# Pairs of experts with at most 32 tokens: 32 slots on four column groups in place of 64 on two

## The chip, the core and the metric

The kernel runs on one core of a Trainium2 chip. The metric is the device time of one execution in microseconds (us). Before the change three runs gave 617.89, 619.68 and 620.88 us; the median is 619.68.

The engines go by the profile's names: PE is the matrix engine and PEld its weight load, DVE, ACT and POOL are the vector, scalar and GpSimd engines, SP issues most DMAs. A letter q behind a name (PEq, PEldq, SPq) is the engine's own sequencer, which fetches and issues its instructions.

## The reference, cut to what matters

The kernel computes one layer over 256 tokens of width 1024. The change touches only its last part, a mixture of 16 experts of inner width 512. A router picks one of four groups of four experts for each token, and two experts in it:

```python
scores = jax.nn.sigmoid(h @ router_w)
sel = scores + router_bias
grp = sel.reshape(sel.shape[:-1] + (N_GROUPS, EXPERTS_PER_GROUP))        # 4 x 4
g_idx = jnp.argmax(jnp.sum(lax.top_k(grp, TOP_K)[0], axis=-1), axis=-1)  # TOP_K = 2
...                                        # e_idx: the two best experts of that group
gate = ...                                 # their scores, normalised, 0 for the others
for e in range(N_EXPERTS):
    he = jax.nn.silu(h @ w1[e]) * (h @ w3[e])
    out = out + gate[..., e:e + 1] * (he @ w2[e])
```

and the layer ends with `xl = xl + g2 * out`. The kernel computes each expert only for the tokens that chose it. With the reference's inputs the fuller expert of each pair (experts 2p and 2p + 1 are pair p) has 55, 42, 15, 14, 49, 72, 29 and 41 tokens, for pairs 0 to 7.

## The kernel before

The part before the experts (up to some 372 us) stays as it is. The experts are worked through in eight pairs. An expert of a pair has 64 slots, so that the 128 partitions hold both: `slots(p, oh, w)` (L1137) makes from a one-hot matrix the slots' transpose `oT` and the gates `gsl` of the slots. `open_group` gathers the tokens of two pairs (`gather`, L1107). Then a pair goes through these steps on PE, each with its line in the rows below:

- `product(p, i, ph)`, L1153 to L1164, the projection w1 (i = 0) or w3 (i = 1): for 8 chunks k of the width and both experts s a matmul with 64 columns (the slots), 512 wide, which fills 64 of 128 partitions of a PSUM bank;
- `silu` on ACT and `weigh` on DVE (gate times silu times the other projection) give `he`; `hidden` (L1173) transposes it on PE;
- `rows` (L1180): the expert outputs, 16 matmuls with 64 columns, 512 wide; `split_rows` writes them as two float32r parts `ys` (ACT and DVE);
- `scatter` (L1190): 16 matmuls with `oT` bring the outputs to the tokens, and DVE adds them to `xl`.

Where an expert has more than 64 tokens, `extra(p, n)` (L1204) does the whole pair again for 32 further slots, with its own matmuls of 32 columns (`phe`, `pye`), and `further` (L1315) repeats this up to 256. Whether this is needed is decided on the chip: `count(p)` (L1308) loads the fuller expert's count from `cnt` into registers of every engine, and `tc.If(counts[p] > 64)` branches on it. `expect(p)` (L1311) puts an early notice of the branch's likely way into PE's stream (BRANCH_PREFETCH_HINT). For pairs 2 to 6 `second` (L1326) puts the second projection into both arms of that branch. So `extra` lies between the branch and the other arm, and a pair that doesn't need it jumps over it.

The order of work on PE is the order of the code (`manual_schedule`); the other engines are ordered by the scheduler. In the loop over p the transposed steps of pair p lie between those of pair p + 1: after the second projection come pair p + 1's slots (and, for odd p, the next group's gather), then `hidden` and `rows` of pair p, two k steps of pair p + 1's first projection, the scatter of pair p, the count, a k step, the notice, and the other five k steps.

The experts' weights are 192 tiles of 512 KB, 24 a pair, in the order of use (`ew_order`, L102). They go through 35 buffers. `load_experts` (L117) issues loads as long as `room` allows, the first 31 on POOL's queue and the others on SP's. `freed(n)` (L1347) gives buffers back in the program's text, 8 for each of a pair's three matrices; a load then still waits on the chip for the matmuls that read its buffer. In pairs 2 to 6 `freed(16)` stands behind the branch, which every engine passes.

PSUM has two pools of banks here: `mm_bank` for projections and half of the transposes, `ax_bank` for the others, with `py` among them.

Pair 7 has its weights cut in another way (`quarter`), so that its products are 256 wide and its outputs come in four quarters (`last_rows(c)`, L1419), each followed by the scatter and the store of the quarter before.

## Time and profile before

| what | value |
| --- | --- |
| median of three runs | 619.68 us (617.89 to 620.88) |
| the profiled execution's own time | 616.12 us |
| its span (first to last instruction) | 614.3 us |
| PE busy | 580.2 us, 94% of the span, 4127 matmuls |
| PEld busy | 408.1 us, 66% |
| DVE / ACT / POOL busy | 349.1 us, 57% / 259.8 us, 42% / 19.4 us, 3% |
| granted PE clock | full in every slice |
| DMA over the span | 170.65 MB, mean 278 GB/s |
| DMA in the expert part | some 407 GB/s in most slices, with a dip to 226 in the one from 538 to 553 us |
| loads of expert weights | 161 on SP's queue (median 10.2 us to landing), 31 on POOL's (7.3 us) |

The profile is one execution; its own time lies 3.6 us under the median of the runs. The rows below are of four kinds. A timeline row is a run of equal instructions of an engine, with its start, its duration and in brackets the idle time before it and what ended that. A windows row gives each engine's busy time in a stretch, the clock, and the share of the stretch in which the 16 DMA engines were busy. A source or tile row lists the instructions of a line or on a tile with least, median and longest duration in ns and the first and last start. And a waits row sums the idle time by what ended it.

### The profile page before, as it was taken

What the parts mean: (1) busy time and instruction counts of PE and PEld (TensorE: products, weight loads), DVE (VectorE), ACT (ScalarE), POOL (GpSimd) and SP (SyncE); (2) the same over time, 40 slices, a digit from 0 to 9 for tenths busy, and PEclk for the clock granted to TensorE, in tenths of its full rate; (3) what the DMA queues carried; (4) which work ended last, traced back from release to release, by engine and by line L of the source; (5) the groups of instructions that cost most, each with busy time, mean ns of one, the idle gap of its engine ahead of it and who ended that gap; (6) DMA issues with size and microseconds to landing.
All of it is one profiled execution on the core that took longest, in us unless ns stands there. A gap on an engine that the chain in (4) does not pass through costs nothing. (4 is left out here: it accounts for less than half of the span.)

```text
span 614.3 us, 10619 instructions
## 1 busy us (share of the span) xinstructions
PE 580.2 (94%) x4127; PEld 408.1 (66%) x4127; DVE 349.1 (57%) x797; ACT 259.8 (42%) x456; POOL 19.4 (3%) x42
## 2 busy tenths in 40 slices
PE   1899999999999899999999988999999999999986
PEld 0789888778788778888899975335445334454454
DVE  4667899999758968988469554121240314132303
ACT  4345446654598765877545624203012111130101
POOL 0000000000000000103112010000000000000000
PEclk9999999999999999999999999999999999999999
DMA  8983874446853463759969776999999999969961
GB/s 256 367 339 114 310 259 154 137 141 193 278 212 103 138 241 103 236 176 356 313 211 379 283 245 226 388 360 406 402 393 407 407 408 409 398 226 409 409 248 68
DMA packets 51825, 170.65 MB, mean 278 GB/s; under 512 B 5664, under 2 KB 10016, under 8 KB 51744
## 3 DMA queue, kind: packets, MB, share of 16 engines
q1 hardware_dynamic: 46704, 151.26, 67.2%
q0 software_dynamic: 5040, 18.35, 8.6%
q8 instruction: 46, 0.75, 0.5%
q14 instruction: 35, 0.29, 0.1%
HBM read 168.54 MB, written 1.05 MB: 276 GB/s over the span
## 5 line engine op out<-in xcount | busy, mean ns | idle before, releaser
L1162 PE MATMUL ph<-ew,xg 128*64 128x512 f32 (+1 forms) x576 | 115.6, 548 | 3.5 <-PEq L1318 2.8
L73 ACT ACTIVATE w<-raw 128x1024 fp32r<-128x1024 f32 x68 | 71.8, 1056 | 65.6 <-PE gps L69 11.6
L74 DVE TENSOR_TENSOR w<-raw,w 128x1024 fp32r<-128x1024 f32 x68 | 82.9, 1219 | 21.5 <-ACT w L73 20.8
L1162 PEld LDWEIGHTS ph<-ew,xg 128*64 128x64 f32 x576 | 41.5, 137 | 66.0 <-issue 58.3
L70 PE MATMUL gps<-h,w 128*128 128x256 f32 x192 | 55.2, 288 | 1.2 <-DVE w L74 1.2
L68 PE MATMUL gps<-h,w 128*128 128x256 f32 x192 | 56.0, 291 | 0.4 <-DVE y L934 0.4
L69 PE MATMUL gps<-h,w 128*128 128x256 f32 x192 | 54.5, 284 | 0.0
L593 DVE SCALAR_TENSOR_TENSOR cacc<-up,vc,cacc 128x243 f32<-128x243 f32 (+14 forms) x120 | 52.1, 472 | 1.4 <-ACT cacc L585 0.7
L1171 DVE SCALAR_TENSOR_TENSOR he<-sl,gsl,ph 128x256 f32<-128x256 f32 x16 | 7.1, 477 | 77.5 <-PE ph L1162 76.2
L1183 PE MATMUL py<-ew,heT 128*64 128x512 f32 x224 | 49.6, 595 | 1.2 <-ACT heT L1178 0.8
L74 DVE TENSOR_TENSOR ys<-py,ys 128x512 fp32r<-128x512 f32 (+1 forms) x18 | 11.4, 633 | 58.0 <-ACT ys L73 58.0
L68 PEld LDWEIGHTS gps<-h,w 128*128 128x128 f32 x192 | 36.6, 191 | 4.2 <-issue 2.6
L70 PEld LDWEIGHTS gps<-h,w 128*128 128x128 f32 x192 | 36.7, 191 | 2.8 <-issue 1.5
L69 PEld LDWEIGHTS gps<-h,w 128*128 128x128 f32 x192 | 36.7, 191 | 0.9 <-issue 0.7
L1183 PEld LDWEIGHTS py<-ew,heT 128*64 128x64 f32 x224 | 15.5, 137 | 30.8 <-issue 26.0
L1201 DVE SCALAR_TENSOR_TENSOR xl<-scp,g,xl 128x256 f32<-128x256 f32 x72 | 29.2, 475 | 7.5 <-PE scp L1197 7.5
L1167 ACT ACTIVATE sl<-ph 128x512 f32<-128x512 f32 (+1 forms) x9 | 5.0, 550 | 63.1 <-PE ph L1162 40.4
L73 ACT ACTIVATE ys<-py 128x512 fp32r<-128x512 f32 (+1 forms) x18 | 9.9, 550 | 50.5 <-PE py L1183 36.6
L114 POOL DMA_DIRECT2D ew<-in_w_exp x31 | 16.6, 537 | 321.1 <-ACT pp L813 248.8
L1119 ACT ACTIVATE xg<-gps,b2m 128x256 f32<-128x256 f32 x32 | 13.4, 471 | 22.7 <-PE gps L1115 21.8
L349 PE MATMUL mps<-ma,cs 128*32 128x256 f32 (+1 forms) x160 | 10.1, 397 | 13.2 <-DMA ma<-in_mod_a 13.1
L1197 PEld LDWEIGHTS scp<-oT,ys 128*128 128x128 f32 x128 | 15.7, 188 | 6.7 <-issue 5.2
(358 smaller groups left out, 1310.0 us busy)
## 6 DMA issues: line engine op xcount, KB each, us to landing
ew<-in_w_exp SPq DMA_DIRECT2D x161, 512.0 KB, 10.2
raw<-in_w_in SPq DMA_DIRECT2D x40, 512.0 KB, 4.4
ew<-in_w_exp POOLq DMA_DIRECT2D x31, 512.0 KB, 7.3
raw<-in_mod_b SPq DMA_DIRECT2D x28, 512.0 KB, 4.1
ma<-in_mod_a SPq DMA_DIRECT2D x12, 512.0 KB, 10.0
raw<-in_w_br SPq DMA_DIRECT2D x12, 512.0 KB, 4.0
raw<-in_w_out SPq DMA_DIRECT2D x8, 512.0 KB, 7.5
ma<-in_mod_a SPq DMA_DIRECT2D x8, 256.0 KB, 6.7
```

The lines of the kernel that those rows point to most:

```text
L68: pe.matmul(ps, wh, xh, start=start, stop=False, skip_group_check=True)
L69: pe.matmul(ps, wh, xl_, start=False, stop=False, skip_group_check=True)
L70: return pe.matmul(ps, wl, xh, start=False, stop=stop, skip_group_check=True)
L73: act.activation(hi, src, AF.Copy)
L74: dve.tensor_tensor(lo, src, r32(hi), op=ALU.subtract)
L114: queue.dma_start(t, w_exp[6 * p + 2 * i + s, :, 1024 * q:1024 * q + 1024])
L593: dve.scalar_tensor_tensor(cacc[:, b, i0:i1], up[:, b, i0 + o:i1 + o], half_d[:, b * 31 + j:b * 31 + j + 1], cacc[:, b, i0:i1], op0=ALU.mu ...
L1119: act.activation(place(k0 + j), ps[:, j, :], AF.Identity, bias=b2m[:, k0 + j:k0 + j + 1])
L1162: pe.matmul(ph[64 * s:64 * s + 64, cols], xg(k)[:, c:c + 64], w[:, at], start=k == 0 and not h, stop=k == KD - 1, skip_group_check=True)
L1183: pe.matmul(py[q][64 * s:64 * s + 64, :], heT[f // 2][:, f % 2, 64 * s:64 * s + 64], ew[p][2][f][s][:, q * 512:q * 512 + 512], start=f == ...
L1197: pe.matmul(ps[:, j, :], rows_(i, m), toks(m), start=(j == 0 and i == 0), stop=i == parts - 1, skip_group_check=True)
L1201: dve.scalar_tensor_tensor(xl[:, m, :], ps[:, j, :], g2[:, m:m + 1], xl[:, m, :], op0=ALU.mult, op1=ALU.add)
```

## The change

The pairs 1 to 6 are now written by a function `pair(p, oT, gsl, toks)`, and each has three branches on the chip.

- **The first**, on count > 32, chooses the first projection: `product` as before, or `product_small`. That uses only the first 32 slots of an expert; the two experts (s) and the two halves of the 512 wide result (h) each take a group of 32 columns, so that 128 partitions hold the whole projection in 256 elements: 32 matmuls with 32 columns, 256 wide, in place of 16 with 64 columns, 512 wide. In this arm POOL clears and fills `oTb` and the upper half of each expert's gates `gsl`, so that the slots stand twice; in the wide arm it copies `oT` to `oTb`.
- **The second**, on count > 64, is the old one, with `extra` and the wide remainder of the pair in its first arm. Its notice (`expect(p)`) stands in both arms of the first branch.
- **The third**, on count > 32 once more, lies in the second one's other arm and chooses between the wide remainder of the pair and the small one: one `weigh`, one `hidden`, and `rows_small`, whose 16 matmuls with 32 columns put both halves of the width into one bank.

Each arm now goes on to the outputs (`rows` and `split_rows`) before the arms meet. `freed(8)`, for the first projection, stands behind the first join, and `freed(16)`, for the second projection and the outputs, behind the second; before, `freed(16)` stood behind the second projection's join and `freed(8)` behind the outputs. The outputs' banks come from `mm_bank`. The scatter is cut in two: the first four of its eight blocks stand behind the next pair's slots and in front of its first branch, the others in the middle of that pair, behind the second projection (`toks` holds `oT` for the first half and `oTb` for the second). The next pair's slots and gather no longer stand between the second projection and `hidden`. For pair 7 the notice of its branch stands in front of its slots. In the changed kernel these functions have lines of their own: `product_small` is L1175, `rows_small` L1204, `hidden` L1189, the scatter L1218, the branches L1398 (first), L1414 and L1340 (the second and its `extra`) and L1421.

```diff
@@ -1163,6 +1163,18 @@
                           stop=k == KD - 1, skip_group_check=True)
             yield
 
+    def product_small(p, i, ph):
+
+
+        xg, xo = group[p // 2][0], p % 2 * 128
+        for k in range(KD):
+            for s in range(2):
+                for h in range(2):
+                    w, at = quarter(p, i, s, k, h)
+                    c = 64 * s + 32 * h
+                    pe.matmul(ph[c:c + 32, :256], xg(k)[:, xo + 64 * s:xo + 64 * s + 32], w[:, at], start=k == 0,
+                              stop=k == KD - 1, skip_group_check=True)
+
     def silu(ph, c=slice(0, 512)):
         act.activation(sl[:, c], ph[:, c], AF.Silu)
 
@@ -1182,6 +1194,15 @@
         for s in range(2):
             pe.matmul(py[q][64 * s:64 * s + 64, :], heT[f // 2][:, f % 2, 64 * s:64 * s + 64],
                       ew[p][2][f][s][:, q * 512:q * 512 + 512], start=f == 0, stop=f == 3, skip_group_check=True)
+
+    def rows_small(p, py):
+
+        for f in range(4):
+            for s in range(2):
+                for q in range(2):
+                    c, x = 64 * s + 32 * q, 64 * s + 32 * (f // 2)
+                    pe.matmul(py[c:c + 32, :], heT[0][:, f % 2, x:x + 32], ew[p][2][f][s][:, q * 512:q * 512 + 512],
+                              start=f == 0, stop=f == 3, skip_group_check=True)
 
     def split_rows(py, q):
         c = slice(q * 512, q * 512 + 512)
@@ -1308,31 +1329,21 @@
     def count(p):
         counts[p] = nc.values_load(cnt[0:1, p:p + 1], min_val=0, max_val=T)
 
-    def expect(p):
-
-        tc.mark_branch_hint_location(f"more{p}", hint=counts[p] > 64, engines=(mybir.EngineType.PE,))
+    def expect(p, n=64):
+
+        tc.mark_branch_hint_location(f"more{p}" if n == 64 else f"more{p}_{n}", hint=counts[p] > n,
+                                     engines=(mybir.EngineType.PE,))
 
     def further(p, n):
 
         if n < T:
-            with tc.If(counts[p] > n, label=f"more{p}" if n == 64 else None):
+            with tc.If(counts[p] > n, label=f"more{p}" if n == 64 else f"more{p}_{n}"):
                 extra(p, n)
                 further(p, n + 32)
 
     def more(p):
 
         further(p, 64)
-
-    def second(p, ph0, ph):
-
-        with tc.If(counts[p] > 64, label=f"more{p}") as c:
-            extra(p, 64, product(p, 1, ph))
-            further(p, 96)
-            silu(ph0)
-        with c.Else():
-            silu(ph0)
-            for _ in product(p, 1, ph):
-                pass
 
     def open_group(g):
         o = one_hot(4 * g)[0] if g else oh0
@@ -1363,42 +1374,102 @@
             more(0)
     oT, gsl = pair_slots(0)
     run(w1)
-    for p in range(7):
-        ph = mm_bank(name="ph1")
-        if p > 1:
-            second(p, ph0, ph)
-            freed(16)
-        else:
-
-            if p:
-                more(p)
-            freed(8 if p else 8 - len(brief))
-            silu(ph0)
-            run(product(p, 1, ph))
-            freed(8)
+    def scatter_rows(toks, ms):
+
+        scatter(lambda i, m: ys[i][:, m * 128:m * 128 + 128], lambda m: toks[m // 4], ms)
+
+    def wide_rows(p, ph, gsl, toks):
+
         for q in range(2):
             weigh(gsl, ph, q)
-        if p % 2:
-            run(open_group(p // 2 + 1))
-        oT_ = oT
-        oT, gsl = pair_slots(p + 1)
-        ph0 = mm_bank(name="ph0")
-        w1 = product(p + 1, 0, ph0, 0 if p == 6 else None)
+        scatter_rows(toks, range(4, 8))
         for q in range(2):
             hidden(q)
-        py = [ax_bank(name="py0"), ax_bank(name="py1")]
+        py = [mm_bank(name="py0"), mm_bank(name="py1")]
         for q in range(2):
             for f in range(4):
                 rows(p, py, f, q)
             split_rows(py, q)
+
+    def pair(p, oT, gsl, toks):
+
+        oTb = work.tile([128, T], F32R, name="oTb", bufs=2)
+        ph0, ph = mm_bank(name="ph0"), mm_bank(name="ph1")
+        with tc.If(counts[p] > 32) as c:
+            w1 = product(p, 0, ph0)
+            ahead(w1, 1)
+            expect(p)
+            run(w1)
+            pool.tensor_copy(oTb, oT)
+        with c.Else():
+            expect(p)
+            product_small(p, 0, ph0)
+
+            pool.memset(r32(oTb), 0.0)
+            for s in range(2):
+                a, b = slice(64 * s, 64 * s + 32), slice(64 * s + 32, 64 * s + 64)
+                pool.tensor_copy(oTb[b], oT[a])
+                pool.tensor_copy(gsl[b], gsl[a])
         freed(8)
-
-        ahead(w1, 2)
-        scatter(lambda i, m: ys[i][:, m * 128:m * 128 + 128], lambda m: oT_)
+        with tc.If(counts[p] > 64, label=f"more{p}") as c:
+            expect(p, 96)
+            extra(p, 64, product(p, 1, ph))
+            further(p, 96)
+            silu(ph0)
+            wide_rows(p, ph, gsl, toks)
+        with c.Else():
+            with tc.If(counts[p] > 32) as d:
+                silu(ph0)
+                run(product(p, 1, ph))
+                wide_rows(p, ph, gsl, toks)
+            with d.Else():
+                silu(ph0, slice(0, 256))
+                product_small(p, 1, ph)
+                weigh(gsl, ph, 0)
+                scatter_rows(toks, range(4, 6))
+                hidden(0)
+                scatter_rows(toks, range(6, 8))
+                py = mm_bank(name="py0")
+                rows_small(p, py)
+                for q in range(2):
+                    split_rows([py, py], q)
+        freed(16)
+        return oT, oTb
+
+
+    ph = mm_bank(name="ph1")
+    freed(8 - len(brief))
+    silu(ph0)
+    run(product(0, 1, ph))
+    freed(8)
+    for q in range(2):
+        weigh(gsl, ph, q)
+    count(1)
+    toks = oT, oT
+    oT, gsl = pair_slots(1)
+    for q in range(2):
+        hidden(q)
+    py = [mm_bank(name="py0"), mm_bank(name="py1")]
+    for q in range(2):
+        for f in range(4):
+            rows(0, py, f, q)
+        split_rows(py, q)
+    freed(8)
+    for p in range(1, 7):
+        if p % 2 == 0:
+            run(open_group(p // 2))
+        if p > 1:
+            oT, gsl = pair_slots(p)
+        scatter_rows(toks, range(4))
+        toks = pair(p, oT, gsl, toks)
         count(p + 1)
-        ahead(w1, 1)
-        expect(p + 1)
-        run(w1)
+    expect(7)
+    oT, gsl = pair_slots(7)
+    ph0 = mm_bank(name="ph0")
+    w1 = product(7, 0, ph0, 0)
+    ahead(w1, 2)
+    scatter_rows(toks, range(8))
+    run(w1)
 
 
     more(7)
```

The stream of PE shows what moved. Of the names, `ph` is a projection's bank, `py` an output's, `hp` the transposed hidden values, `scp` the scatter's, `ohp` and `pg` those of the slots and the gates, and xN at the end is a count of instructions (the trace has two records, and two weight loads, for each of the matmuls with float32 operands, and one for a transpose or for a matmul with float32r, as in the scatter); the number behind a name tells one bank from another of that name.

**PE, the end of pair 2 and the start of pair 3.** Before, behind the join of pair 2's second projection:

```order
L1328 UNCONDITIONAL_BRANCH
L1141 MATMUL ohp<-ident,oh 128x128 x2
L1146 MATMUL pg<-gate,oh 128x2 x2
L1177 MATMUL hp<-ident,he 128x128 x4
L1183 MATMUL py_7848<-ew,heT 64x512 x8
L1183 MATMUL py_7849<-ew,heT 64x512 x8
L1162 MATMUL ph_7839<-ew,xg 64x512 x4
L1197 MATMUL scp<-oT,ys 128x256 x16
```

Now pair 2 has an arm of its own, which stands behind the jump that ends the wide arm (the first row of code, L1175, is its second projection):

```order
L1175 MATMUL ph_6938<-ew,xg 32x256 x32
L1218 MATMUL scp<-oTb,ys 128x256 x4
L1189 MATMUL hp<-ident,he 128x128 x2
L1218 MATMUL scp<-oTb,ys 128x256 x4
L1204 MATMUL py_8170<-ew,heT 32x512 x16
L1421 UNCONDITIONAL_BRANCH
L1330 TENSOR_LOAD cnt
L1141 MATMUL ohp<-ident,oh 128x128 x2
L1146 MATMUL pg<-gate,oh 128x2 x2
L1218 MATMUL scp<-oT,ys 128x256 x8
```

The next pair's slots (L1141, L1146) moved from in front of the transposes to behind the outputs, the outputs (L1204) are one row of 16 in place of two of 8, and the old scatter's row of 16 became four pieces: two of 4 for the pair before, around the transposes, and one of 8 for this pair, behind the join. (The other 8 come in pair 3.)

**PE, the branches of pair 3.** Before, from the load of the count on (the rows behind the branch are the start of `extra`):

```order
L1309 TENSOR_LOAD cnt
L1162 MATMUL ph_7839<-ew,xg 64x512 x2
L1313 REGISTER_ALU
L1541 BRANCH_PREFETCH_HINT
L1162 MATMUL ph_7839<-ew,xg 64x512 x10
L1328 COMPARE_AND_BRANCH
L1220 MATMUL gpe<-hT,ohe 128x512 x8
L1141 MATMUL ohp<-ident,ohe 128x128 x2
```

Now:

```order
L1398 COMPARE_AND_BRANCH
L1162 MATMUL ph_8263<-ew,xg 64x512 x2
L1334 REGISTER_ALU
L1612 BRANCH_PREFETCH_HINT
L1162 MATMUL ph_8263<-ew,xg 64x512 x14
L1398 UNCONDITIONAL_BRANCH
L1334 REGISTER_ALU
L1612 BRANCH_PREFETCH_HINT
L1175 MATMUL ph_8263<-ew,xg 32x256 x32
L1398 UNCONDITIONAL_BRANCH
L1414 COMPARE_AND_BRANCH
```

Before there was one branch, with its notice ten matmuls ahead of it. Now there are two in a row ahead of `extra`, with a notice in each arm of the first, 14 matmuls of 512 wide or 32 of 256 wide ahead of the second; the third, on L1421, stands behind `extra` and the arm that goes with it.

**PE, the end of pair 6 and the branch of pair 7.** Before, from the first four matmuls of pair 7's first projection on:

```order
L1162 MATMUL ph_12573<-ew,xg 64x256 x4
L1197 MATMUL scp<-oT,ys 128x256 x16
L1309 TENSOR_LOAD cnt
L1162 MATMUL ph_12573<-ew,xg 64x256 x2
L1313 REGISTER_ALU
L1541 BRANCH_PREFETCH_HINT
L1162 MATMUL ph_12573<-ew,xg 64x256 x10
L1318 COMPARE_AND_BRANCH
```

Now:

```order
L1330 TENSOR_LOAD cnt
L1334 REGISTER_ALU
L1612 BRANCH_PREFETCH_HINT
L1141 MATMUL ohp<-ident,oh 128x128 x2
L1146 MATMUL pg<-gate,oh 128x2 x2
L1162 MATMUL ph_13633<-ew,xg 64x256 x4
L1218 MATMUL scp<-oT,ys 128x256 x8
L1218 MATMUL scp<-oTb,ys 128x256 x8
L1162 MATMUL ph_13633<-ew,xg 64x256 x12
L1340 COMPARE_AND_BRANCH
```

The notice of pair 7's branch (L1541, now L1612) moved from ten matmuls ahead of the branch to ahead of the slots, the scatter and all sixteen.

## Rows read from the trace of the kernel before

**Rows 1.** Busy time by stretch (header: us, instructions in brackets), expert part

```profile
core 0: us, PE busy (x) PEld busy (x) DVE busy (x) ACT busy (x) POOL busy (x), PEclk, DMA share, GB/s
416.00:520.00 104.00, 103.10 (x544) 46.84 (x540) 24.70 (x64) 17.82 (x40) 0.00 (x0) 1.00 1.02 405
...
535.00:545.00 10.00, 9.15 (x66) 5.31 (x59) 4.79 (x11) 2.46 (x6) 0.00 (x0) 1.00 0.46 161
```

**Rows 2.** Expert weight loads on SP: 416 to 520, 517.3, 584.3 us

```profile
L114 SPq DMA_DIRECT2D ew<-in_w_exp x79: 327/328/586, 416.6 to 519.9; - x79
...
L114 SPq DMA_DIRECT2D ew<-in_w_exp x1: 328/328/328, 517.3 to 517.3; - x1
...
DMA to landing us min/median/max: 10.2/10.2/10.2
...
L114 SPq DMA_DIRECT2D ew<-in_w_exp x1: 327/327/327, 584.3 to 584.3; - x1
...
DMA to landing us min/median/max: 11.8/11.8/11.8
```

**Rows 3.** Waits of SP's queue (total us, times, longest)

```profile
SPq L114 <- PEq L1318: 18.8, 3, 9.3
```

**Rows 4.** PE's timeline, pair 7 (start, us, line, shape, count, [idle before])

```profile
582.49 2.81 PE L1162 MATMUL ph<-ew,xg 128*64 128x256 f32 x24
587.91 7.13 PE L1162 MATMUL ph<-ew,xg 128*64 128x256 f32 x64 [2.61 <-PEq L1318]
...
606.65 1.95 PE L1419 MATMUL py<-ew,heT 128*64 128x256 f32 x16
```

**Rows 5.** The same, pair 2's outputs to pair 4's gather

```profile
447.36 0.89 PE L1177 MATMUL hp<-ident,he 128*128 128x128 f32 x4
448.33 7.09 PE L1183 MATMUL py<-ew,heT 128*64 128x512 f32 x32
455.24 1.89 PE L1162 MATMUL ph<-ew,xg 128*64 128x512 f32 x8
457.06 2.15 PE L1197 MATMUL scp<-oT,ys 128*128 128x256 f32 x16
459.14 12.24 PE L1162 MATMUL ph<-ew,xg 128*64 128x512 f32 x56
471.31 4.07 PE L1115 MATMUL gps<-oh,hT 128*128 128x256 f32 x32
```

**Rows 6.** The same, pair 5's extra slots

```profile
522.17 7.11 PE L1241 MATMUL phe<-ew,heT 128*32 128x256 f32 x128
...
531.08 0.44 PE L1249 MATMUL hpe<-ident,he 128*128 128x128 f32 x2
...
532.46 3.64 PE L1258 MATMUL pye<-ew,heT 128*32 128x512 f32 x32
```

**Rows 7.** Branches and hints on PE's sequencer: pairs 2, 5, 7

```profile
L1541 PEldq BRANCH_PREFETCH_HINT  x1: 40/40/40, 432.9 to 432.9; - x1
...
L1328 PEldq COMPARE_BRANCH  x1: 3524/3524/3524, 435.4 to 435.4; - x1
...
L1318 PEldq COMPARE_BRANCH  x1: 3341/3341/3341, 538.5 to 538.5; - x1
...
L1328 PEldq COMPARE_BRANCH  x1: 187/187/187, 542.1 to 542.1; - x1
...
L1541 PEldq BRANCH_PREFETCH_HINT  x1: 40/40/40, 581.6 to 581.6; - x1
...
L1318 PEldq COMPARE_BRANCH  x1: 4750/4750/4750, 583.0 to 583.0; - x1
```

**Rows 8.** Instruction loads and matmul counts, 50 to 360 us

```profile
q8 instruction: 17, 0.28, 0.4%
...
50.00:360.00 310.00, 305.68 (x2285) 262.30 (x2284) 252.48 (x511) 192.82 (x311) 16.58 (x31) 1.00 0.64 218
```

**Rows 9.** A POOL operation on 128 by 128 (us, ns | idle before)

```profile
L257 POOL IOTA jp<- 128x128 int32 x1 | 0.2, 225 | 0.4 <-POOLq L1549 0.4
```


## Prediction

> **What bounds the kernel now.** I read the stretches first, then PE's timeline, then the branches, the weight loads and SP's waits. The change touches only the expert part, from about 401 us on. There two engines are full at once. Over 416 to 520 us PE is busy for 103.1 of 104.0 us, and the DMA share is 1.02 [rows 1]. Weights arrive at one tile of 512 KB per 1.32 us: 79 issues between 416.6 and 519.9 us [rows 2]. A pair has 24 tiles, so 31.8 us of transfer, while PE needs 24 us from pair 2's transposes (447.36) to the end of pair 3's projections (471.31), and 4 more where a gather comes [rows 5]; DMA is the slower one, and PE lives on tiles loaded ahead. That turns round at pair 5, the only pair that goes through `extra`: PE stays in it so long that the buffers fill, and from 535 to 545 us the DMA share is 0.46 [rows 1]. So (1.02 - 0.46) / 1.02 x 10 us = 5.5 us of transfer time is lost there, with SP waiting at PE's join (9.3 us, the longest of its kind) [rows 3]. The last tile is issued at 584.3 us and lands 11.8 us later, at 596.1 [rows 2]; PE begins the last quarter's rows only at 606.65 [rows 4]. At the end, then, PE is late by some 10 us, and it sets the end. PE has few holes: the reader should see the one of 2.61 us in pair 7 behind a branch [rows 4].
>
> **What the change removes.** It concerns three pairs: the counts put 2, 3 and 6 on the new arm; 1, 4 and 5 stay wide, 0 and 7 lie outside `pair`. In a wide pair the two projections take 1.89 + 12.24 us, the expert outputs 7.09 and the four transposes 0.89 [rows 5]. The arm for at most 32 tokens has the forms that `extra` has today: 128 matmul records of 32 columns, 256 wide, in 7.11 us, 32 records 512 wide in 3.64, two transposes in 0.44 [rows 6]. So a small pair saves 14.13 - 7.11 = 7.02, 7.09 - 3.64 = 3.45 and 0.45, together 10.9 us of PE, three pairs 32.8.
>
> **What it adds: branches on PE.** A pair now has three branches, and a small pair jumps at each. What a jump costs is read from PE's sequencer. The jump over the `extra` code of pair 2 takes from its hint at 432.9 us to the branch's end at 435.4 + 3.5 = 438.9, which is 6.0 us; in pair 7 it is 581.6 to 583.0 + 4.75 = 587.75, 6.2 us [rows 7]. In pair 2 it lies beneath the scatter's end and the wide products behind it and costs nothing. In pair 7 the products are half as wide, and what isn't covered is the 2.61 us hole. Without a hint the jump at 538.5 us took 3.34, and a short one at 542.1 took 0.19 [rows 7].
> - The middle branch, far, hinted: in a small pair the hint stands directly in front of the 32 small products, 3.5 us. Of the 6.2 us, 2.7 stay open, less up to 1.5 us of work that PE still has queued at the hint (its sequencer is that far ahead: pair 7's branch begins at 583.0, the products in front of it run to 585.3). Between 1.2 and 2.7 I take 1.7, the nearer to the queued case, since the half scatter stands in front. In wide pairs a product of 7 us covers it.
> - The third branch, not hinted, over the wide arm, directly behind the far jump, with nothing to cover it. That arm is 152 records: 32 products at four (two matmuls, two weight loads), 12 transposes and scatter matmuls at two. If the target has been loaded it costs 0.2, else 3.34. In straight code PE loads a block 17 times in 310 us for 2285 + 2284 records, one in 269 [rows 8]; 152 of 269 jumps, 57 in 100, leave the block just loaded: 2.0 us, kept open from 0.2 to 3.5.
> - The first branch jumps over 66 records, in code that runs straight and behind queued work: 0, up to 0.7. The wide pairs' jump to the join lies under the outputs' 7 us: nothing.
>
> Jumps per small pair, then: J = 1.7 + 2.0 = 3.7 us, between 1.4 and 6.9.
>
> The trace shows loads on jumps, but not which jumps are free of one. The Trainium skill, "Runtime: NRT & Kernel Launch", section "Instruction fetch mechanics", says that a taken branch forces a fetch only if its target is outside a window of two pages. The far jump agrees with it (3.3 to 4.75 us). By it the third branch, whose target is at most one page on, would be free and J 1.9; the first rival is built on this.
>
> **What it moves.** The second half of a pair's scatter now stands between the projections and the transposes, in the place of the next pair's slots, gather and first products, which hid the weighing on DVE. Two weighings stand against half a scatter, 1.1 us [rows 5]. I estimate 0.5 us more per pair, and in a small pair 0.5 us more for the outputs' split at its start: 3 us for pairs 1 to 5, 2.5 for the rest, bounds 0 and twice that. POOL gets five small operations per small pair; the only POOL rows like them are of 0.2 us [rows 9]. DVE needs the gates 7 us later, so even 1 us each is hidden. Outputs in other banks cost nothing I can see: no PE wait on a bank stands in front of them today. The hint of pair 7 moves ahead of the slots, the scatter (2.15) and all sixteen products (16/12 x 2.81 = 3.75 [rows 4]), 5.9 us of PE work and the slots on top, so the 2.6 us hole closes; if not, 2.6 us are lost again. The loads of the second projection's and the outputs' tiles are now issued behind the pair's join in the program, but wait for the same products; cost 0, or 5 us if SP has to wait for the join as it did in pair 5.
>
> **The sum, against the profiled execution.** PE can't use its gain fully, because in pairs 3 to 5 it runs into the weights. Transfers run without a hole up to pair 5, so tiles come no earlier than now. Pair 5's last tile is the one issued at 517.3, landing at 527.5 [rows 2]. PE ends the rows that need it at 536.1 now (532.46 + 3.64 [rows 6]), so at most 527.9 then: a gain of at most 8.2 us at this point, while pairs 2 and 3 offer 2 x (10.9 - 3.7) - 3 = 11.4. So 8.2, and the jumps of pairs 2 and 3 disappear in waiting. Behind it: pair 6 gives 10.9 - 3.7 = 7.2, pair 7's hole 2.6, the moved waits cost 2.5. Sum 8.2 + 7.2 + 2.6 - 2.5 = 15.5 us.
>
> The other limit is the last tile: without pair 5's hole it lands at 596.1 - 5.5 = 590.6. From the start of the last quarter's rows to the span's end are 614.3 - 606.65 = 7.65 us. So the span is no less than 598.3, a gain of 16.0. Both limits meet. I take 15.0, since the two seldom fit without a little waiting: span 599.3. The profiled execution took 616.12 us, 1.8 more than its span and 3.6 under the median of the runs, 619.68; I carry the difference over: 619.7 - 15.0 = 604.7, say 605.
>
> **The rivals.** With J per small pair the gain is min(8.2, 18.8 - 2J) + 10.9 - J + 0.1, and no more than 16.0.
> - **The third branch costs next to nothing, and weights alone set the end** (J under 3.2). Gain 16.0: 603.7, with some jitter 602 to 605. For it: the DMA share of 1.02, and that the short jump at 542.1 cost 0.19. Against: that one followed loaded code, and this one follows a jump. Chance 0.25. (It is the case in which the rule of "Instruction fetch mechanics" in the Trainium skill's "Runtime: NRT & Kernel Launch" holds to the letter.)
> - **Code loads take a good part back** (J of 5.5 to 8, the first jump or the second page missing too). Gain 7.8 + 5.4 + 0.1 = 13.3 at J = 5.5, down to 5.8 at J = 8: 606.4 to 613.9, at J = 6.5 609.4. For it: the longest jump took 4.75 us, and it was one under a full DMA. Chance 0.2.
> - **Slower: the jumps cost more than the narrow products save.** The place is PE's stream in pairs 2, 3 and 6; it decides from 18.8 - 2J + 11.0 - J = 0, J = 9.9. With 2.7 open behind the hint, and three unhinted loads at 3.34 to 4.75, at the first branch, the third and the page behind it, J = 12.7 to 17; at 12.7 the gain is -8.3: 628. For it: nothing stands between these branches. Against: one short jump cost 0.19. Chance 0.07.
> - **The arm isn't taken,** the counts being other than I worked out: all pairs wide, the moved waits cost 5.5, the hole gives 2.6: 622.6. The trace agrees with the counts in that `extra` ran once, in pair 5. Chance 0.02.
>
> **How the numbers follow.** My own case has 0.46: 603 to 607. The range from 600 (the weights' case with 4 us of jitter) to 613 holds that, the first rival and most of the second, 0.87; beyond it lie the second's tail, the slower one and the last. I lower this to 0.84 for causes I haven't listed. From no change a measurement can tell about 0.5%, 3.1 us. Faster by more: 0.25 + 0.46 + 0.18 = 0.89, less those 0.03, so 0.86. Within: 0.02 of the second's tail and the 0.03, 0.05. Slower: 0.07 + 0.02 = 0.09.
>
> **What would show it.** Records of line 1175 in pairs 2, 3 and 6, about 3.5 us each; a hole on PE put down to its own sequencer before the second small projection, 3 to 5 us in all; PE waiting for weights in pairs 3 to 5; no DMA hole at 535 to 545 us; the last tile landing near 591, and the last quarter's rows beginning within 2 us of it; no 2.6 us hole in pair 7. It would be wrong if the DMA share falls below 1 in pairs 1 to 4 (SP waiting for joins), or if the holes at the branches exceed 5 us per small pair.

## Result and profile after

The changed kernel takes 633.96 us (median of 4 runs, 632.39 to 635.40) against 620.00 for the kernel before: ratio 1.0241, 95% interval 1.0206 to 1.0276. It is slower by 14.0 us, where 605 was forecast. Times are medians of a kernel's runs; in run 10 below one execution of twelve took 1096.9 us and is left out.

| | before | after |
| --- | --- | --- |
| profiled execution, its span | 616.12, 614.3 us | 634.45, 632.7 us |
| mean granted PE clock | 0.999 | 0.972 |
| expert part: pair 0's slots to the last matmul's end | 382.6 to 610.2 | 387.3 to 628.7 |
| PE busy in it | 220.7 us | 200.6 us |
| PE idle in it (holes over 0.1 us) | 6.3 us | 40.2 us |
| last weight tile lands [rows 2] | 596.1 us | 610.7 us |
| last quarter's rows begin [rows 4] | 606.65 us | 625.16 us |

The expert part is 13.8 us longer, about as much as the medians differ. (It also begins 4.7 us later in this pair of executions. The kernels run below begin it between 384.4 and 389.2 us, and with the instructions of before up to there it was 384.5 once, so part of this belongs to the execution; the medians don't contain it as a whole. How much the change adds there stays open.) PE's busy time did fall, by 20.1 us, and its holes grew by 33.9.

PE's timeline of the kernel after, pairs 1 to 4 and 5 to 7 (start, us, line, shape, count, in brackets the idle time ahead and what ended it; "issue" is time for which the profile shows no releaser):

```profile
415.73 8.78 PE L1162 MATMUL ph<-ew,xg 128*64 128x512 f32 x32 [1.99 <-issue]
...
439.65 3.66 PE L1175 MATMUL ph<-ew,xg 128*32 128x256 f32 x64
453.82 5.43 PE L1175 MATMUL ph<-ew,xg 128*32 128x256 f32 x64 [10.51 <-issue]
...
461.06 3.64 PE L1204 MATMUL py<-ew,heT 128*32 128x512 f32 x32
...
467.29 3.66 PE L1175 MATMUL ph<-ew,xg 128*32 128x256 f32 x64
481.40 5.30 PE L1175 MATMUL ph<-ew,xg 128*32 128x256 f32 x64 [10.45 <-DMA ew<-in_w_exp]
...
506.95 7.09 PE L1162 MATMUL ph<-ew,xg 128*64 128x512 f32 x32 [1.99 <-issue]
...
568.13 4.04 PE L1115 MATMUL gps<-oh,hT 128*128 128x256 f32 x32 [2.17 <-issue]
...
581.18 3.17 PE L1175 MATMUL ph<-ew,xg 128*32 128x256 f32 x28 [3.14 <-issue]
586.43 3.81 PE L1175 MATMUL ph<-ew,xg 128*32 128x256 f32 x36 [2.08 <-issue]
...
605.09 2.13 PE L1162 MATMUL ph<-ew,xg 128*64 128x256 f32 x17 [2.36 <-PEq L1340]
608.13 5.40 PE L1162 MATMUL ph<-ew,xg 128*64 128x256 f32 x47 [0.91 <-issue]
```

The reader is to see that the narrow forms cost about what was read from `extra` [rows 6], 3.66 us a projection and 3.64 for the outputs, and that in front of the second projection of each small pair PE stands still: 10.51, 10.45 and 3.14 us, in pair 6 2.08 more in the middle of it. The wide pairs 1 and 4 have new holes of 1.99, and pair 7 still has one [rows 4], now in two pieces. Pair 3's hole is put down to a weight tile, but its third branch ends at 481.2, 0.2 us before the products begin, so the branches explain it without one.

PE's sequencer in pair 2, then in pair 6 (L1612 is the notice, L1398, L1414 and L1421 the three branches; ns, then the start):

```profile
L1398 PEldq COMPARE_BRANCH  x1: 341/341/341, 438.6 to 438.6; - x1
...
L1612 PEldq BRANCH_PREFETCH_HINT  x1: 40/40/40, 439.1 to 439.1; - x1
...
L1414 PEldq COMPARE_BRANCH  x1: 6056/6056/6056, 441.9 to 441.9; - x1
...
L1421 PEldq COMPARE_BRANCH  x1: 5632/5632/5632, 448.0 to 448.0; - x1
...
L1414 PEldq COMPARE_BRANCH  x1: 4142/4142/4142, 576.6 to 576.6; - x1
...
L1421 PEldq COMPARE_BRANCH  x1: 228/228/228, 580.8 to 580.8; - x1
```

Two branches in a row of 6.06 and 5.63 us, 11.7 together, of which the queued work covers 1.2: that is the hole. Pair 3 has 6.02 and 5.65. In pair 6 the third branch took 0.23. PE's code comes through the queue q8 "instruction" [rows 8]; three of its loads in pair 2, in stretches of one us from 442.2, 445.3 and 451.1 us (packets, MB, share of the stretch):

```profile
q8 instruction: 1, 0.02, 7.4%
...
q8 instruction: 1, 0.02, 6.7%
...
q8 instruction: 1, 0.02, 6.9%
```

They start at 442.29, 445.38 and 451.20. The second is 3.5 us behind the start of the middle branch, which ends 2.5 us after it; the third is 3.2 us behind the start of the third branch, which ends 2.5 us after it. So the code behind both branches is asked for only when they are reached, and the notice at 439.1 shows no effect. The first load, by a count of the code's records, was asked for when PE entered a new block at the jump of 438.6, and brings the block behind that, which isn't needed; this is a reading, the trace doesn't say what a load brings.

The clock and the weights, in two stretches of the kernel after: pair 2's hole with the products behind it, and pair 3's:

```profile
core 0: us, PE busy (x) PEld busy (x) DVE busy (x) ACT busy (x) POOL busy (x), PEclk, DMA share, GB/s
...
443.00:458.00 15.00, 4.49 (x53) 2.30 (x49) 0.00 (x0) 0.38 (x1) 0.00 (x0) 0.66 0.64 249
...
471.00:486.00 15.00, 4.60 (x56) 2.62 (x60) 0.00 (x0) 0.39 (x1) 0.00 (x0) 0.66 1.02 405
```

In the holes the granted clock falls from 2.4 to 1.2 GHz (1.00 to 0.50, in pair 2 at some 447.2 us, with PE idle since 443.3) and is back only at some 457.5, with PE at work since 453.8: the second projection takes 5.43 us instead of 3.66. And the DMA share falls to 0.64 there, as SP waits for PE's products (its longest such wait, on L1175, is 12.7 us); the last tile lands 14.6 us later than before. Both things that the prediction called signs of being wrong are there: a DMA share below 1 in pairs 1 to 4, and holes of over 5 us per small pair.

### The profile page after: what moved, and what is told of

Same layout as the page of the kernel before. It is cut to its first block, busy times and chain, and to the rows that moved or that the text cites. A ratio compares the mean times of both kernels' runs of the same rounds, so it can differ in the third digit from the quotient of the medians.

```text
span 632.7 us, 11092 instructions
## 1 busy us (share of the span) xinstructions
PE 562.0 (89%) x4313; PEld 407.2 (64%) x4313; DVE 348.6 (55%) x794; ACT 257.6 (41%) x453; POOL 25.2 (4%) x60
## 5 line engine op out<-in xcount | busy, mean ns | idle before, releaser
L73 ACT ACTIVATE w<-raw 128x1024 fp32r<-128x1024 f32 x68 | 71.8, 1057 | 69.7 <-DMA raw<-in_w_in 13.8
L1162 PE MATMUL ph<-ew,xg 128*64 128x512 f32 (+1 forms) x384 | 74.8, 535 | 7.2 <-issue 4.9
L1162 PEld LDWEIGHTS ph<-ew,xg 128*64 128x64 f32 x384 | 28.8, 138 | 44.2 <-issue 38.6
L1175 PE MATMUL ph<-ew,xg 128*32 128x256 f32 x384 | 28.7, 454 | 26.2 <-issue 15.7
L1175 PEld LDWEIGHTS ph<-ew,xg 128*32 128x32 f32 x384 | 14.6, 128 | 38.8 <-issue 33.2
L1190 ACT ACTIVATE heT<-hp 128x256 f32<-128x256 f32 x13 | 4.8, 383 | 73.9 <-PE hp L1189 73.8
L1195 PE MATMUL py<-ew,heT 128*64 128x512 f32 x128 | 28.3, 595 | 0.8 <-ACT heT L1190 0.6
L1179 ACT ACTIVATE sl<-ph 128x256 f32<-128x256 f32 (+1 forms) x9 | 4.3, 479 | 49.7 <-PE ph L1162 22.4
L349 PE MATMUL mps<-ma,cs 128*32 128x256 f32 (+1 forms) x160 | 10.1, 397 | 13.8 <-DMA ma<-in_mod_a 13.8
```

Source lines behind the costliest of these rows:

```text
L73: act.activation(hi, src, AF.Copy)
L349: pe.matmul(self.ps[c:c + 32, :], cs[:, 2 * n + j, :], ma[self.i][n][:, j, o:o + self.w], start=n == 0, stop=n == KD // 2 - 1, skip_group_ ...
L1162: pe.matmul(ph[64 * s:64 * s + 64, cols], xg(k)[:, c:c + 64], w[:, at], start=k == 0 and not h, stop=k == KD - 1, skip_group_check=True)
L1175: pe.matmul(ph[c:c + 32, :256], xg(k)[:, xo + 64 * s:xo + 64 * s + 32], w[:, at], start=k == 0, stop=k == KD - 1, skip_group_check=True)
L1195: pe.matmul(py[q][64 * s:64 * s + 64, :], heT[f // 2][:, f % 2, 64 * s:64 * s + 64], ew[p][2][f][s][:, q * 512:q * 512 + 512], start=f == ...
```

## Experiments

The theories, as they stood after this profile. **A, blocks of code:** PE's code comes in blocks, taken as 256 records (one load for 269 in [rows 8], and the places where the products of pairs 6 and 7 break off fit it); PE holds the block it is in and one other; when it enters a block it asks for the next; a jump to neither waits 3.4 us for the load's start and 2.5 more. A notice helps only if its load can still be asked for in time. **B, weights:** loads issued behind the joins come late and set the time. **C, the clock** alone eats the gain. Each run was timed beside the kernel before; ratios are to it, with the 95% interval.

**1. No pair is small.**

```diff
-        with tc.If(counts[p] > 32) as c:
+        with tc.If(counts[p] > 8) as c:
...
-            with tc.If(counts[p] > 32) as d:
+            with tc.If(counts[p] > 8) as d:
```

> The limit of 32 tokens in the first and third branch becomes 8, so that no pair takes the narrow arms; all else is as in the changed kernel. Theory A (blocks of code): PE's code comes in blocks of 256 records; PE holds the block it is in and one more, asks for the next block when it enters one, and a jump elsewhere costs some 5.9 us less what is queued. The wide pairs then have holes of about 2 us at the middle branch in pairs 1, 4 and 6, none in 2 and 3, 2.2 behind pair 5 and about 3.3 in pair 7: PE's work is that of the kernel before and the time 628 to 634 us. Theory B (weights): the loads issued behind the joins come late and set the time of the changed kernel; 33 us more of PE work then come on top of late weights, 640 us or more. Theory C (the clock alone costs the gain): no long holes, no slow clock, 622 us.

Measured 632.51 us, ratio 1.0208 (1.0177 to 1.0240). Holes of 1.9 us behind the middle branch came in pairs 1, 4 and 6, and, unexpected, in pair 2; 2.1 behind pair 5. Pair 7 had 0.9 in two pieces, where 3.3 were expected. The scaffold of branches and moves costs as much as the narrow products save: with them and without them the kernel takes the same. PE has 27 us more to do (busy 227.6 against 200.6) and nothing gets slower; B had 640 or more, though by this run alone another bound could still hide the work. Run 4 settles that.

**2. The branch on 32 outside the one on 64.**

```diff
-        with tc.If(counts[p] > 64, label=f"more{p}") as c:
...
+        with tc.If(counts[p] > 32, label=f"far{p}") as c:
+            with tc.If(counts[p] > 64, label=f"more{p}") as d:
...                                  # extra and wide; else wide
+        with c.Else():
...                                  # the small arm, as it was
```

> The second and third branch change places: the branch on 32 stands outside and the one on 64 inside its wide arm, so that a small pair jumps once, straight to its arm, with the notice in the small arm of the first branch given for this jump. A: the second load of code goes, 5.6 us in pair 2, some 4 in pair 3 (a block ends within the small products), nothing in pair 6, and the clock gives 2 or 3 back: 619 to 626 us, with one hole of 5 us in front of the second small projection of pairs 2 and 3. B: no change within 3 us, 631 to 637, and the hole is filled by a wait for weights. C: as A for the hole, but the products behind it still run at 1.2 GHz.

Measured 624.13 us, ratio 1.0102 (1.0054 to 1.0150). PE's timeline:

```profile
443.29 6.37 PE L1175 MATMUL ph<-ew,xg 128*32 128x256 f32 x64 [4.83 <-issue]
...
465.95 5.29 PE L1175 MATMUL ph<-ew,xg 128*32 128x256 f32 x64 [4.64 <-issue]
```

The hole halves in both pairs: one of its two loads is gone. The time is within what A said, but the products behind the hole still run slow (6.37 and 5.29 us for 3.66), as C had it and A had not.

**3. The notice in front of the slots.**

```diff
+        expect(p)
         if p > 1:
             oT, gsl = pair_slots(p)
...
-            expect(p)                    # in both arms of the first branch
```

> The notice of the branch on 64 moves out of both arms of the first branch to in front of the pair's slots. A: in pairs 2 and 3 the code of the middle jump is asked for when PE enters the block before it, not behind a load that isn't wanted: the middle branch ends 3 us earlier, the third costs its 5.6 as before; in pairs 1 and 4, where a block ends in the jump over the small arm, nothing changes. 626 to 630 us. B: 632 to 636, no change. A rival within A, that notices do nothing here wherever they stand: no change either, and the middle branch still takes 6 us in pairs 2 and 3.

Measured 627.15 us, ratio 1.0118 (1.0076 to 1.0159). Middle and third branch of pairs 2 and 3:

```profile
L1411 PEldq COMPARE_BRANCH  x2: 2815/2882/2948, 439.5 to 465.1; - x2
...
L1418 PEldq COMPARE_BRANCH  x2: 5678/5846/6015, 442.5 to 468.0; - x2
```

The middle branch is 3.1 us shorter, the third unchanged, the holes of pairs 1 and 4 unchanged (1.8 and 2.0). So a notice can work here, and where it stands decides; by A it works where its load isn't asked for behind another.

**4. Instructions that never run.** This run executes what the changed kernel executes and nothing else: the traces have the same number of instructions, 11092, and the same of each kind.

```diff
+        for _ in range({2: 32, 3: 47, 6: 40}.get(p, 0) if n == 224 else 0):   # in extra
+            pe.matmul(py[0:32, :], heT[0][:, 0, 0:32], ew[p][2][0][0][:, 0:512], start=True, stop=True,
```

> Only instructions that are never executed are added, 32, 47 and 40 matmuls in the deepest extra of pairs 2, 3 and 6 (128, 188 and 160 records). They shift the target of the middle jump to the first records of a block, so that the target of the third branch lies in the same block. A: the third branch falls from 5.6 us to some 0.2 in pairs 2 and 3, and a new hole of 2 to 3 us comes within the second small projection, where the block ends; holes also go in pairs 4 and 7, whose notice and branch then lie otherwise to the blocks' ends. 618 to 626 us. B, C and any theory by executed work: 632 to 636, no change.

Measured 618.05 us, ratio 0.9973 (0.9947 to 0.9999): 15.9 us less than the changed kernel, by moving code alone. Third branch and second projection of pair 2:

```profile
L1424 PEldq COMPARE_BRANCH  x1: 229/229/229, 446.0 to 446.0; - x1
...
446.37 5.34 PE L1175 MATMUL ph<-ew,xg 128*32 128x256 f32 x46 [5.11 <-issue]
451.88 1.65 PE L1175 MATMUL ph<-ew,xg 128*32 128x256 f32 x18 [0.17 <-issue]
```

The third branch fell from 5.63 to 0.23 us (pair 3: 5.65 to 0.22). The products now break off where the block was to end, at 46 of 64, for 0.17 us here and 1.0 in pair 3, less than the 2 to 3 expected, probably because at the lower clock PE reaches that place late. From the target to the break lie the 152 records of the wide arm, 46 products and their 46 weight loads, 244, and some records of branches and semaphores, which fits a block of 256. The hole of pair 4 and the second piece of pair 7's are gone; its first piece, 2.5 us, stayed. No theory by executed work can give this: that the place of the code makes the holes is shown. The details of A (two blocks held, the next asked for on entering one) fit most branches here, not run 1's in pair 2, and were not varied one by one.

**5. Runs 2 and 3 together**, the small pairs' notice in front of the slots.

```diff
+        expect_small(p)                  # notice of the jump far{p}
         if p > 1:
             oT, gsl = pair_slots(p)
```

> The branch on 32 outside the branch on 64 (as in the run with the other nesting, 624.1 us), and the notice of a small pair's jump in front of its slots; the wide arm's notice stands at its start. A (blocks of code): the hole in front of the second small projection of pair 2 shrinks from 4.8 to under 2, that of pair 3 by 2 to 3, wide pairs as before: 617 to 621 us. Rival, that a notice is worth nothing in front of another branch: 623 to 625.

Measured 620.96 us, ratio 1.0026 (1.0002 to 1.0051). The holes of pairs 2 and 3 are 1.87 and 1.63, and the products behind them are back at 3.66 us each, at the higher clock. What is left lies in pairs 1 (1.76), 4 (2.78), 6 and 7 and behind pair 5 (2.46).

**6. The same, aligned by instructions that never run**, placed by counting records.

```diff
+        for _ in range({0: 39, 1: 36, 2: 49, 3: 44, 4: 23, 5: 35}.get(p, 0) if n == 224 else 0):
+            pe.matmul(py[0:32, :], heT[0][:, 0, 0:32], ew[p][2][0][0][:, 0:512], start=True, stop=True,
```

> The same with instructions that are never executed, 39, 36, 49, 44, 23 and 35 matmuls in the deepest extra of pairs 0 to 5, chosen so that each notice lies in the block of its branch, or ahead of the only block's end before it, and each small arm within one block. A: no hole of more than 2.5 us behind a branch, no slow clock in the expert part, 604 to 611 us; PE then meets the weights, whose last tile lands at some 592 us. Rival, that the weights' loads behind the joins have been the limit for some time: 614 us or more, with PE waiting for tiles.

Measured 606.07 us, ratio 0.9782 (0.9747 to 0.9817). This version beats both kernels, the one before by 13 us. Pair 2, then the issue and landing of the last tile, then the last quarter's rows:

```profile
440.24 3.66 PE L1175 MATMUL ph<-ew,xg 128*32 128x256 f32 x64 [1.79 <-issue]
...
L114 SPq DMA_DIRECT2D ew<-in_w_exp x1: 328/328/328, 588.4 to 588.4; - x1
...
DMA to landing us min/median/max: 10.0/10.0/10.0
...
598.99 1.95 PE L1495 MATMUL py<-ew,heT 128*64 128x256 f32 x16
```

The tile lands at 598.4 us and the quarter that needs it begins 0.6 us later: now the two limits meet, as the prediction had them. The transfers run without a hole (DMA share 1.00 to 1.03 from 416 to 588 us), another of its signs, but the tile lands 7.8 us behind the 590.6 of its sum; the expert part begins 3.8 us later in this execution (386.4 for 382.6), and the rest stays open. Two details missed: pair 4 kept a hole of 2.6, and in pair 6 a hole of 2.07 was followed by the lower clock.

**7. The kernel before with one part of the change**, pair 7's notice in front of its slots.

```diff
         oT_ = oT
+        if p == 6:
+            count(7)
+            expect(7)
         oT, gsl = pair_slots(p + 1)
...
-        expect(p + 1)                    # for p < 6 it stays
```

> The kernel before, with one part of the change alone: the count and the notice of pair 7's branch in front of its slots. A: between notice and branch a block ends some 78 records behind the notice, well before the branch, so the jump's code is asked for there and the hole of 2.6 us goes: 615.8 to 617.5 us against 619.0. Rival, that the notice does nothing there, as in the changed kernel, where 2.4 us of that hole stayed: 618.5 to 619.5.

Measured 616.47 us, ratio 0.9960 (0.9937 to 0.9984). The products behind the branch, to be held against [rows 4]:

```profile
588.44 7.31 PE L1162 MATMUL ph<-ew,xg 128*64 128x256 f32 x64 [0.16 <-PEq L1318]
```

So this part of the change is worth the 2.6 us that were put on it, in the layout of before. In the changed kernel, by the count of records, a block ended some 15 records ahead of the branch; its load starts only at 602.35, within the branch (600.4 to 604.9), though the notice came at 593.5.

**8. The aligned kernel with fewer weights.** The second and third matrix of pair 4 are not loaded, the first stands in for them; the result is that of other weights.

```diff
+    ew_order = [x for x in ew_order if x[0] != 4 or x[1] == 0]
...
+        if p == 4:
+            ew[4][1] = ew[4][2] = ew[4][0]
```

> As the aligned kernel, but the second and third matrix of pair 4 are not loaded: its first matrix is used in their place, so 16 tiles of 512 KB, 21 us of transfer, are left out, with PE's work unchanged. If the weights set the end of the aligned kernel, this one is faster by 4 to 10 us, until PE alone is the bound; if PE's work and its holes set it, the two agree within 2 us.

Measured 601.46 us, ratio 0.9704 (0.9665 to 0.9744), 4.6 us less than run 6. Its last tile lands at 592.0 us and its last quarter begins at 595.84: PE sets the end here, so in run 6 the weights cost about the difference.

**9. The aligned kernel, no pair small** (both limits 8, as in run 1).

> The aligned kernel (606.1 us) with the limit of 32 tokens at 8, so that no pair takes the narrow arms. A: PE's work is that of the kernel before, the holes at branches are gone; what remains against the kernel before is the moved scatter and weighing, and the hole of pair 7: 616 to 621 us, so the narrow arms by themselves bring 10 to 15 us. Rival, that the order of work and the alignment brought the gain and the narrow arms little: 606 to 612.

Measured 625.56 us, ratio 1.0094 (1.0065 to 1.0124), which misses both. The kernel without the narrow arms is 5 to 10 us slower than I said, and 19.5 us slower than run 6 (625.56 - 606.07). But not all of this is due to the arms. The trace shows a part that isn't, the notice and the branch of pair 7, and the products behind them.

```profile
L1617 PEldq BRANCH_PREFETCH_HINT  x1: 40/40/40, 585.2 to 585.2; - x1
...
L1346 PEldq COMPARE_BRANCH  x1: 6179/6179/6179, 589.8 to 589.8; - x1
...
596.16 4.11 PE L1162 MATMUL ph<-ew,xg 128*64 128x256 f32 x18 [4.04 <-PEq L1346]
```

The code is that of run 6 but for the two limits, and there this branch took 0.35 us with its notice at 570.6. Here pair 6 is wide and ends with a jump that lands at 584.7, the next block is asked for (load at 588.03), the notice comes 0.5 us later and is lost: the branch asks for itself (load at 593.46, 3.65 us behind its start). It is the case of pairs 2 and 3 of the changed kernel. So a notice that comes while another load is awaited does nothing; that is read from these three places (439.1, 466.8 and this one) and was not tried by a run of its own. The hole of 4.04 and the 64 products behind it, 9.86 us and at first at the lower clock, stand against 0.16 and 7.28 in run 6: 6.5 us. So by an estimate the narrow arms themselves bring some 13 of the 19.5, within the 10 to 15 expected.

**10. The aligned kernel without the small pairs' notice.**

```diff
-        expect_small(p)
```

> The aligned kernel without the notice of the small pairs' jump; the wide arm's notice stays. A: each of the three jumps then asks for its code itself, 3.4 us and 2.5 more to its landing, less what is queued: holes of some 5 us in pairs 2, 3 and 6 in place of 1.6 to 2.1, and the slow clock behind them: 615 to 620 us. Rival, that where the code lies matters and the notice doesn't: 606 to 609.

Measured 615.09 us, ratio 0.9942 (0.9909 to 0.9974). The branch of pairs 2 and 3 and the products behind it in each:

```profile
L1418 PEldq COMPARE_BRANCH  x2: 6058/6105/6152, 435.1 to 457.4; - x2
...
441.29 5.89 PE L1175 MATMUL ph<-ew,xg 128*32 128x256 f32 x64 [4.77 <-issue]
...
469.53 5.43 PE L1175 MATMUL ph<-ew,xg 128*32 128x256 f32 x64 [10.66 <-DMA ew<-in_w_exp]
```

Against run 6 the branch takes 6.1 us for 3.0, so the aligned kernel needs the notice too. But pair 3's hole is 10.66, where some 5 were expected. Its branch ended at 463.6, PE's sequencer passed the wait for the weight tile there in 0.05 us, and one weight load of PE followed; the products went on 2.55 us behind the start of a further load of code (466.98). The edit takes the notices' records out and so shifts all code behind them, and in pair 3 a block seems to end just behind the jump's target now. So the 9 us between the two runs are not the price of the notices alone: the notice is worth some 3 us at a branch, and the rest is the lost alignment and the lower clock.

## Why the prediction was wrong, by its own steps

**What failed first is the price J of the jumps ("What it adds: branches on PE").** It was put at 3.7 us for each small pair, between 1.4 and 6.9. Measured are 10.5, 10.5 and 5.2 (3.14 + 2.08), 26.2 us where 11.1 were expected.
- *The middle branch*, 1.7, rests on the 6.2 us from notice to landing [rows 7]. The notice was lost, so the 6.2 count from the branch itself and no product covers them. Run 3 gave 3.1 us back by the notice's place alone.
- *The third branch*, 2.0, was a chance of 57 in 100 times 3.34. It is no matter of chance: it was 5.6 in pairs 2 and 3, where by the count of records the target lay beyond the block's end, and 0.23 in pair 6, where it didn't. And 3.34 [rows 7] was not a whole load: the load that ended it started 1.0 us behind the branch, so it had been asked for before. A whole one takes 5.3 to 6.2. Run 2 removed this load, and run 4 removed it without touching any executed instruction.
- *The first branch*, 0: right, 0.34 us.
- *What no term had*: a block that ends soon behind a jump (pair 6's 2.08, pair 7's 0.91).

**"In wide pairs a product of 7 us covers it" failed too**: pairs 1 and 4 have holes of 1.99, because the notice there had no effect either and the branch took 5.74, in pair 1:

```profile
L1414 PEldq COMPARE_BRANCH  x1: 5739/5739/5739, 409.7 to 409.7; - x1
```

Behind pair 5 the jump over the small arm left 2.17, where before the join left 0.85.

**The clock was left out.** With holes that long PE ran at the lower level behind them: second projections of 5.43, 5.30 and 3.17 + 3.81 instead of 3.66, and 8.78 for 7.09 in pair 1, 8.4 us together. That is the larger part of why PE's busy time fell by 20.1 and not by 32.8. Where the holes of pairs 2 and 3 were short, in runs 5 and 6, the products behind them ran at the higher clock, so there the clock followed from the holes and C is no cause of its own.

**How the terms add up.** On PE's side, without the weights' limit, the forecast was 32.8 - 11.1 - 5.5 + 2.6 = 18.8 us gained. The 15.1 that J cost beyond its price would alone have left a gain of 3.7. The holes of the wide pairs and behind pair 5 take 5.3 (2 x 1.99 + 2.17 - 0.85), the clock 8.4, and pair 7's hole 3.3 (2.36 + 0.91), where none was expected: in sum a loss of 13.3, where the expert part is 13.8 longer. So J was the largest single miss, and the others made a loss of what was left.

**Right by mechanism:** the narrow forms (3.66, 3.64, 0.44), which pairs take the arm, the moved waits roughly (0.53 in front of the half scatter and 0.3 in front of the outputs; by the timeline some 3.7 us of new waits, 5.5 expected), the weights as the second limit, and pair 7's hole, whose 2.6 us run 7 found, but not in the layout that the change gives. The term 8.2 for the meeting with the weights never came into play, since PE was late everywhere; in run 6 PE waits for tiles in pairs 3 and 4, so there it did. There J is 1.6 to 2.1, the rival with J under 3.2 had 603.7, and 606.07 was measured.

**The rivals.** The slower one named the right mechanism, loads at several of these branches ("nothing stands between these branches"), and its 628 was nearest; with 0.07 its chance was too small. That it came so near is partly luck: its J of 12.7 a pair was too high (8.7 measured on average), it had a load at the first branch, where none came, and it had neither the wide pairs' holes nor the clock. What should have raised it: two far branches that follow each other can't both be covered by one product, and the trace of before showed no jump into unloaded code without its notice. The rule of the Trainium skill ("Runtime: NRT & Kernel Launch", "Instruction fetch mechanics"), that a taken branch forces a load only outside the window of two blocks, agrees with the runs: 0.23 inside, 5.3 to 6.2 outside where no notice helped. I read it as making the third branch free, since its target is at most one block on. But the runs look as if only one block is there directly behind a far jump: the other seems to be asked for on arrival (in pair 6 the jump ends at 580.7 and the next load starts at 584.11), and the third branch waits 5.6 us for it.

## What to carry to other kernels

Where branches on the chip skip long code, count the records of the code: which block a jump's target and its notice lie in decides between 0.2 and 6 us, and shifting code that never runs moved this kernel by 16 us. Let a short path jump once, straight to its arm, give the notice some 6 us ahead, not just behind another jump, and let no block end between it and the branch. Then compare any two versions of such a kernel only with the layout in mind, since an edit anywhere ahead shifts every branch behind it: runs 9 and 10 read wrongly without that.

## What the runs showed that was not expected

- A load of code that a branch asks for itself takes 5.3 to 6.2 us until PE's sequencer goes on (3.0 to 3.8 to the load's start, some 2.5 from there); behind pair 5 it was 6.5 in run 5 and 7.0 in run 3.
- In the expert part all holes of 3.1 us and more had products at the lower clock behind them; one of 2.0 did in pair 1 (8.78 us) and an equal one in pair 4 did not (7.09); run 6 had it again behind 2.07 in pair 6.
- A notice of a branch is not a reservation: at 439.1, 466.8 and, in run 9, 585.2 us it had no effect, each time within 0.6 us of a jump into a block whose successor was, by the count of records, just being asked for.
